# Token mean squares by a constant stationary operand: a root of 528 columns instead of a root of five and a spreading by transposition

## The chip, the cores and the metric

The kernel runs on one core of a Trainium2 chip. The metric is the device time of one execution in microseconds (us); lower is better. Times before are 818.12, 819.78 and 821.24 us, with a median of 819.78. One further execution was profiled: it took 818.42 us, and the profile's span, from its first instruction to its last, is 816.4 us.

## The reference

Two layers of an encoder with a residual stream of 528 tokens (512 of a grid, 16 meta tokens) by 1024 features. What matters here is the norm at the start of each layer, the projection behind it, and the norm of each head's queries and keys:

```
def rms_norm(x, g):
    xf = x.astype(jnp.float32)
    y = xf * lax.rsqrt(jnp.mean(xf * xf, axis=-1, keepdims=True) + EPS)
    return (y * g.astype(jnp.float32)).astype(x.dtype)

h = rms_norm(x, norm_g)
proj = jnp.einsum('bld,de->ble', h, w_in)
qa, ka, va, za, qb, kb, vb, zb, ga, gb = split_cols(proj)
qa = apply_axial_rope(rms_norm(qa.reshape(b, l, ATTN_HEADS, HEAD_DIM), q_norm_g), cos, sin)
ka = apply_axial_rope(rms_norm(ka.reshape(b, l, ATTN_KV_HEADS, HEAD_DIM), k_norm_g), cos, sin)
```

After that come grouped-query attention over all tokens (branch A), attention over windows of the grid (branch B), gates, output products and the residual sum; behind the second layer a last norm.

## The kernel before, in words

Activations lie with features on the 128 partitions and tokens along the row, 528 columns. Weights come from memory in halves of 128x512 (`weights`, L294): ScalarE rounds each to `whi` (L303), GpSimd subtracts to get the rest, `wlo` (L304). Both have five buffers, so a new half waits until TensorE has finished with the one five places earlier. A product (L379) takes two halves for each block of 128 output columns: per 128 rows of weights three matmuls, `whi` by the high part of the activations, `whi` by the low part, `wlo` by the high part (L388 to L390). In layer 0 a product runs in two spans, columns 0 to 256 and 256 to 528, each in its own bank of `pp`, of which there are two; in layer 1 most products have one span of 512 columns, but those for keys and values still have two. Layer 0's first three products are made in another way while the input arrives (L509).

The order of projections in a layer is QA to QA+3 (queries of branch A), KA (keys), VA (values), and then KB, QB, VB, ZB and ZA for each of four pairs of heads of branch B, then the gates.

The projections are made of the not yet normalized activations times the gain `norm_g`. The inverse root of the mean square of each token is multiplied in when a product leaves PSUM: `rbc`, 128x528, holds it for each token (column), the same on all partitions. Queries and keys of branch A don't use it: each head has a norm of its own, so the token's factor cancels, except that EPS must be added with the right weight, and for that the mean square itself, `mx`, is needed again.

This is how `rbc` comes about before the change:

- The squares of the features are summed over the eight tiles of features, and `norm_split` (L631) splits the sum, 128x528, into a high and a low part, `ssh` and `ssl`.
- `norm_root` calls `inverse_rms` (L433). For each of five blocks of 128 tokens, the last one overlapping the fourth, the slice of `ssh`, and then of `ssl`, is the stationary operand and the constant `mean_d` (128x2, each element 1/1024) is the moving one (L441). Tokens come out on the partitions. VectorE adds EPS (L445), which gives `mx`, 128x5; GpSimd raises it to the power -0.5 (`rsqrt`, L264 to L267), which gives `rx`, 128x5.
- `norm_spread` (L643) turns `rx` back: five transposes of one column broadcast over 128 (L646, L649), and two copies of ScalarE out of PSUM into `rbc` (L647, L650).

The head norms are near it: `sum_squares` (L537) accumulates the squares of the queries and keys into `mh` in PSUM, ten rows of 528 columns. `head_means` (L698) copies them out as `msb`, `head_roots` (L702) transposes that into `mt`, five blocks of 128 tokens by ten heads, adds `mx` times EPS (L712), and takes the roots, those of the keys by the power on GpSimd and those of the queries by Newton steps on VectorE.

What sets the order: each engine has one queue and runs it in order. `tick` (L373) is called after each span of a product, and in layer 1 also in the middle of one, and emits what is due; `NORM_AT` (L42) says after how many ticks the parts of the norm come. On top of that `BEHIND` (L66) lists pairs "this instruction behind that one" for each engine's queue, and `queue_order` (L106) puts them in as dependencies that wait for nothing and only fix the order. SP's pairs are for its DMA queue. `meta_columns` (L637), four small copies on GpSimd (`qmt`), is tied behind the root.

Of the kernel before, what the change touches and what calls it, by code (L numbers as in the profile page):

```python
# [11 lines left out]
F32 = mybir.dt.float32  # L12
# [6 lines left out]
P = 128  # L19
# [19 lines left out]
NA_AT = ({"stages": (0, 2, 4, 5, 5, 7), "values": (3, 4), "divide": (3, 4, 7)},  # L39
         {"stages": (0, 2, 4, 5, 5, 7), "values": (3, 4), "divide": (3, 4, 7)})  # L40

NORM_AT = ({"tokens": (0, 2, 4), "squares": (1, 1, 2, 3, 2), "heads": (2, 3, 5, 7, 6), "values": (1, 4)},  # L42
           {"tokens": (1, 3, 5), "squares": (2, 2, 2, 3, 2), "heads": (2, 3, 5, 7, 6), "values": (1, 4)})

PAIR_AT = (16, 32, 48)
GQA_AT_TICK, NA_AT_TICK = (0, 0), (1, 1)
# [19 lines left out]
BEHIND = {  # L66
    "Activation": (
# [5 lines left out]
    ),  # L73
    "DVE": (
# [6 lines left out]
    ),  # L81
# [11 lines left out]
    ),  # L93
    "Pool": (
        ("KB1_20", 0, "za1_0", 0), ("ga0", 7, "wlo0_24_0", 0), ("ga0", 51, "wlo1_36_1", 0), ("ga0", 52, "wlo1_36_1", 0),
        ("wl6KB", 1, "gb0", 0), ("wlo0_17_1", 0, "zb0_1", 0), ("wlo0_21_0", 0, "ga0", 10), ("wlo1_38_1", 0, "zb1_3", 0),
    ),
    "SP": (
        ("KB0_21", 0, "KB0_21", 1), ("KB0_30", 0, "QB0_3a", 1), ("P0_1_0", 1, "P0_1_0", 3), ("P1_0_0", 1, "P1_0_0", 3),
        ("Q20_1", 2, "KB0_11", 0), ("QB0_3a", 0, "QB0_3a", 1), ("raw1_46_0", 0, "bias1_7", 0), ("turn1_2_1", 0, "QB1_2a", 0),  # L100
        ("turn1_4_1", 0, "bias1_7", 0),
    ),
}
# [52 lines left out]
def trunk_kernel(ctx: ExitStack, tc: tile.TileContext, xT, w, gn, gf, bias, rope, out):  # L156
# [28 lines left out]
    def bank(pool, name, tag):  # L185
        return pool.tile([P, 512], F32, tag=tag, name=name)
# [77 lines left out]
    def rsqrt(out, x):  # L264
        with tc.high_priority():
            e = minus_half.unsqueeze(2) if len(x.shape) == 3 else minus_half
            return nc.gpsimd.tensor_tensor(out, x, e.to_broadcast(list(x.shape)), op=ALU.pow)  # L267
# [157 lines left out]
    def token_tiles(n):  # L425
        return [P * t for t in range(4)] + ([LAST] if n > NREAL else [])
# [3 lines left out]
        split(sh[:, :n], sl[:, :n], ss[:, :n])  # L430
        return sh, sl

    def inverse_rms(ss, n, name):  # L433

        tt = token_tiles(n)
        k = len(tt)
        sh, sl = ss
        ps = bank(ps_t, f"ms{name}", "tp")
        for t, a in enumerate(tt):
            for i, v in enumerate((sh, sl)):  # L440
                nc.tensor.matmul(ps[:, 2 * t:2 * t + 2], v[:, a:a + P], mean_d, start=i == 0, stop=i == 1)  # L441
        mx = tiny.tile([P, 5], F32, tag="mx", name=f"mx{name}")
        rx = tiny.tile([P, 5], F32, tag="rx", name=f"rx{name}")
        with tc.high_priority():
            nc.vector.tensor_scalar_add(mx[:, :k], ps[:, :2 * k].rearrange("p (t i) -> p t i", i=2)[:, :, 0], EPS)  # L445
        return mx, rx, rsqrt(rx[:, :k], mx[:, :k])


    pieces, xs, h, done = {}, [], [], [None, None]
# [72 lines left out]
    for l in range(DEPTH):  # L522
# [109 lines left out]
            st["ss"] = split_squares(total["ss"], NTOK, f"{l}")  # L632

        def norm_root():
            st["mx"], st["rx"], st["root"] = inverse_rms(st["ss"], NTOK, f"{l}")

        def meta_columns():  # L637

            with tc.issue_after(st["root"].ins):
                for j in range(4):  # L640
                    nc.gpsimd.tensor_copy(qmeta[:, j], qs[j][:, NREAL:])

        def norm_spread():  # L643
            ps = bank(ps_t, f"rb{l}", "tp")
            for t in range(4):
                nc.tensor.transpose(ps[:, P * t:P * (t + 1)], st["rx"][:, t:t + 1].to_broadcast([P, P]), ident)  # L646
            nc.scalar.copy(rbc[:, :NREAL], ps)  # L647
            ps = bank(ps_t, f"rbm{l}", "tp")
            nc.tensor.transpose(ps[:, :P], st["rx"][:, 4:5].to_broadcast([P, P]), ident)  # L649
            nc.scalar.copy(rbc[:, NREAL:], ps[:, P - NMETA:P])  # L650

        Q2, qmeta = [None] * 8, tiny.tile([P, 4, NMETA], F32, tag="qmt", bufs=1, name=f"qmt{l}")

# [6 lines left out]
        for j in range(4):  # L660
            q, rotate = rotated(QA + j, g_q[l], full, "q")
            qs.append(q)

            if l == 0:
                turns.append(rotate)
            else:
                with tc.issue_after(evac["low"].ins):
                    rotate()
                if j > 1:
                    stack_pair(j - 2)  # L670
            if l == 0 and j == 3:
                turns[0]()
            if l == 0 and j == 1:

                with tc.issue_after(evac["last"].ins):
                    norm_split()
                evac["last"] = split_at["hi"]
            if j == 0:
                for after, part in zip(NORM_AT[l]["tokens"], (norm_split, norm_root, norm_spread)):
                    if after:  # L680
                        side_gqa.later(after, part)
                if full:
                    side_gqa.later(4, meta_columns)
# [13 lines left out]

        def head_means():  # L698
            st["msb"] = slot("G", f"msb{l}")
            nc.scalar.copy(st["msb"][:10], joined(mps)[:10])  # L700

        def head_roots():  # L702

            ps = bank(ps_a, f"mt{l}", "avn")
            for t, a in enumerate(token_tiles(NTOK)):
                nc.tensor.transpose(ps[:, 10 * t:10 * t + 10], st["msb"][:10, a:a + P], ident[:10, :10])
            mh = tiny.tile([P, 50], F32, tag="mh", bufs=1, name=f"mh{l}")
            rh = tiny.tile([P, 50], F32, tag="rh", bufs=1, name=f"rh{l}")
            m3, st["r3"] = (t.rearrange("p (t c) -> p t c", t=5) for t in (mh, rh))
            p3 = ps[:, :50].rearrange("p (t c) -> p t c", t=5)  # L710
            e3 = st["mx"].unsqueeze(2).to_broadcast([P, 5, 10])
            nc.vector.scalar_tensor_tensor(m3, e3, EPS, p3, op0=ALU.mult, op1=ALU.add)  # L712
            rsqrt(st["r3"][:, :, 8:10], m3[:, :, 8:10])

            r, x = (t[:, :, 0:8] for t in (st["r3"], m3))
            tm = tiny.tile([P, 5, 8], F32, tag="tmh", bufs=1, name=f"tmh{l}")
            nc.vector.tensor_scalar(r.bitcast(I32), x.bitcast(I32), -0.5, float(0x5f3759df), op0=ALU.mult, op1=ALU.add)
            with tc.issue_after(newton(r, x, tm).ins):
                st["fk"] = pair_factors(slice(0, 4), slice(8, 10), 4, "k")
                st["fm"] = pair_factors(slice(4, 5), slice(8, 10), 1, "km")  # L720
            for _ in range(2):
                newton(r, x, tm)
            st["r8"] = tiny.tile([P, 4, 8], F32, tag="r8", name=f"r8_{l}")
            nc.vector.tensor_scalar_mul(st["r8"], r[:, 0:4], 0.125)
# [660 lines left out]
```

## Time and profile before

| what | value |
|---|---|
| median of three runs | 819.78 us |
| profiled execution, time | 818.42 us |
| profiled execution, span | 816.4 us |
| TensorE (PE) busy | 808.9 us |
| VectorE (DVE) busy | 505.5 us |
| ScalarE (ACT) busy | 473.6 us |
| GpSimd (POOL) busy | 418.5 us |
| mean granted clock of TensorE | 0.999 |

How to read what is quoted below. In the page, an engine's line gives its busy time, the share of the span and the number of instructions; then comes the chain of work that ended last. A list of waits has the instruction that waited, what it waited for, and us in total, times, longest us. In the answers for one line of the kernel the three numbers after the count are the shortest, median and longest duration in ns, then the first and last start. In a timeline each row has the start in us from the start of the span, the length in us, engine, line, operation, output and inputs, shapes and count, and in brackets how long the engine had been idle before it and what ended that. L304 is line 304 of the kernel before. Names such as `wlo` or `rx` are those of the program's tiles, without buffer numbers. A matmul's row lasts longer than its share of the engine, since matmuls overlap: the time that it takes is the distance to the start of the next one.

### The profile page before, as it was taken

To read this page: it belongs to the slowest core of one execution; us is meant where nothing else is said; L and a number is where in the kernel's file an instruction comes from. 1 tells how busy PE (TensorE), PEld (TensorE's weight loads), DVE (VectorE), ACT (ScalarE), POOL (GpSimd) and SP (SyncE) were. 2 spreads that over 40 slices of the span, in tenths; PEclk is the share of its full clock that TensorE was granted. 3 is DMA by queue.
4 is the path that set the end of the run, shared out by engine and by line. 5 is a ranking of instruction groups with operands and counts; after the bars stand their busy time and mean duration, and the time that the engine had idled before them with its cause. 6 is when DMAs were issued, how large, how long until landed. Compare 5 with 4: busy or idle time off the path is not lost.

```text
span 816.4 us, 16080 instructions
## 1 busy us (share of the span) xinstructions
PE 808.9 (99%) x5658; PEld 755.5 (93%) x5658; DVE 505.5 (62%) x1154; ACT 473.6 (58%) x1137; POOL 418.5 (51%) x362
## 2 busy tenths in 40 slices
PE   9999999999999999999999999999999999999997
PEld 9999999999999999999998989898988888888886
DVE  7566767796785662456447667676867655344633
ACT  7745677577865664433445557566848755544322
POOL 1654454454553544655764645454725555545750
PEclk9999999999999999999999999999999999999999
DMA  8347574667555563425555584767774555652502
GB/s 299 105 130 210 154 203 134 186 214 203 178 157 181 160 211 118 151 97 172 145 128 133 139 240 135 212 172 189 192 226 162 171 179 155 192 192 90 194 1 104
DMA packets 113248, 134.99 MB, mean 165 GB/s; under 512 B 31888, under 2 KB 66192, under 8 KB 113168
## 3 DMA queue, kind: packets, MB, share of 16 engines
q1 hardware_dynamic: 112448, 132.90, 54.7%
q8 instruction: 45, 0.74, 0.4%
q10 hardware_dynamic: 720, 1.06, 0.3%
q14 instruction: 35, 0.29, 0.1%
HBM read 98.50 MB, written 21.84 MB: 147 GB/s over the span
## 4 chain that ended last, share of the span: by engine, by line
PE 93%; DMA 3%; SPq 1%; issue 1%; DVE 1%; ACT 0%; POOLq 0%; POOL 0%; DVEq 0%
PE pp L390 20%; PE pp L389 20%; PE pp L388 20%; PE av L974 4%; PE y L388 4%; PE y L390 4%; PE y L389 4%; PE avb L1121 2%; PE S L624 2%; PE S L625 2%; PE pf L1305 2%; PE pf L1303 2%; PE pf L1304 2%; PE pp L513 1%; PE Sb L625 1%; PE Sb L624 1%
## 5 line engine op out<-in xcount | busy, mean ns | idle before, releaser
L304 POOL TENSOR_TENSOR wlo<-raw,whi 128x512 fp32r<-128x512 f32 x210 | 285.7, 1370 | 283.2 <-ACT whi L303 224.3
L388 PE MATMUL pp<-hh,whi 128*128 128x256 f32 (+2 forms) x1040 | 325.2, 313 | 0.0
L390 PE MATMUL pp<-hh,wlo 128*128 128x256 f32 (+2 forms) x1040 | 324.3, 312 | 0.0
L389 PE MATMUL pp<-hl,whi 128*128 128x256 f32 (+2 forms) x1040 | 323.4, 311 | 0.0
L390 PEld LDWEIGHTS pp<-hh,wlo 128*128 128x128 f32 x1040 | 195.7, 188 | 10.2
L389 PEld LDWEIGHTS pp<-hl,whi 128*128 128x128 f32 x1040 | 195.7, 188 | 9.4
L388 PEld LDWEIGHTS pp<-hh,whi 128*128 128x128 f32 x1040 | 195.8, 188 | 8.7
L303 ACT CAST whi<-raw 128x512 fp32r<-128x512 f32 x210 | 127.9, 618 | 104.8 <-PE pp L389 42.2
L967 POOL TENSOR_TENSOR ga<-pm,ga 32x128 fp32r<-32x128 f32 x64 | 39.1, 612 | 62.3 <-ACT ga L965 38.4
L936 DVE STREAM_TRANSPOSE P<-P 128x512 f32<-128x512 f32 x64 | 46.3, 725 | 28.5 <-ACT P L910 28.0
L1200 DVE TENSOR_TENSOR mg<-pp,rbc 128x256 f32<-128x256 f32 (+2 forms) x48 | 24.7, 515 | 48.8 <-PE pp L390 48.4
L906 DVE CUSTOM_DVE_ANT_0 P<-S,r 128x528 f32<-128x528 f32 x64 | 44.8, 700 | 14.0 <-PE S L625 13.2
L257 DVE TENSOR_TENSOR ptl<-P,pth 128x512 fp32r<-128x512 f32 x64 | 49.0, 781 | 4.8 <-ACT pth L256 4.2
L910 ACT ACTIVATE P<-P,st 128x528 f32<-128x528 f32 x64 | 47.2, 737 | 1.7
L1061 ACT ACTIVATE bias<-bias,stb 128x208 f32<-128x208 f32 (+1 forms) x64 | 31.0, 485 | 17.9 <-DVE stb L1059 17.8
L1201 ACT ACTIVATE mg<-mg 128x256 f32<-128x256 f32 (+2 forms) x48 | 23.6, 492 | 29.9 <-DVE mg L1200 29.5
L256 ACT CAST pth<-P 128x512 fp32r<-128x512 f32 x64 | 39.3, 613 | 0.9 <-DMA P<-turn 0.8
L389 PE MATMUL pp<-mx,whi 128*128 128x272 f32 (+1 forms) x128 | 36.4, 285 | 0.0
L388 PE MATMUL pp<-mx,whi 128*128 128x272 f32 (+1 forms) x128 | 36.4, 285 | 0.0
L390 PE MATMUL pp<-mx,wlo 128*128 128x272 f32 (+1 forms) x128 | 36.4, 285 | 0.0
L909 ACT ACTIVATE st<-st 128x1 f32<-128x1 f32 x64 | 12.9, 202 | 39.5 <-DVE st L906 38.9
L974 PE MATMUL av<-pth,VA 128*128 128x256 f32 x128 | 34.0, 288 | 0.0
(534 smaller groups left out, 1718.2 us busy)
## 6 DMA issues: line engine op xcount, KB each, us to landing
raw<-in_w_dram SPq DMA_DIRECT2D x210, 256.0 KB
turn<-P SPq DMA_DIRECT2D x32, 528.0 KB
P<-turn SPq DMA_DIRECT2D x128, 128.0 KB
bias<-in_bias_dram SPq DMA_DIRECT2D x16, 480.0 KB
KB<-KB SPq DMA_DIRECT2D x24, 272.0 KB
rawl<-in_w_dram SPq DMA_DIRECT2D x16, 256.0 KB
x<-in_xT_dram SPq DMA_DIRECT2D x8, 264.0 KB
xr<-in_xT_dram SPq DMA_DIRECT2D x8, 264.0 KB
```

The lines of the kernel that those rows point to most:

```text
L256: split_at["hi"] = nc.scalar.copy(hi, src)
L257: split_at["any"] = nc.vector.tensor_sub(lo, src, hi.bitcast(F32))
L303: cast = nc.scalar.copy(hi, raw)
L304: sub = nc.gpsimd.tensor_sub(lo, raw, hi.bitcast(F32))
L388: nc.tensor.matmul(ps, wh, rh[:, a:b], start=i == 0, stop=False)
L389: nc.tensor.matmul(ps, wh, rl[:, a:b], start=False, stop=False)
L390: nc.tensor.matmul(ps, wl, rh[:, a:b], start=False, stop=i == n - 1)
L906: newest["max"] = nc.vector.tensor_tensor_reduce(p[:n], joined(S)[:n], scale[:n].to_broadcast([n, NTOK]), 1.0, -3e38, ALU.mult, ALU.max, s ...
L910: nc.scalar.activation(p[:n], p[:n], AF.Exp, bias=st[:n, 1:2], scale=1.0, accum_out=st[:n, 2:3] if total is None else total)
L936: nc.vector.transpose(c["both"][:n, a:b], c["both"][:n, a:b])
L967: nc.gpsimd.tensor_sub(tm[64 + 32 * t:96 + 32 * t, n * t:n * (t + 1)], m, tm[:32, :n].bitcast(F32))
L974: nc.tensor.matmul(c["av"], rows2(c["t"][i][0]), c["t"][i][1], start=i == 0, stop=i == 8)
```

## The change

`inverse_rms` no longer brings tokens to partitions. The constant, broadcast to 128x128, is the stationary operand, and `ssh` and `ssl` are the moving ones: four matmuls, for columns 0 to 256 and 256 to 528. The mean square of a token then stands in its column on all 128 partitions. VectorE adds EPS in two instructions into `m`, 128x528, a tile of the tag "G" (eight buffers shared with other work), and GpSimd raises all 528 columns to the power -0.5 straight into `rbc`. `norm_spread` and its two ticks go. The mean squares for the heads' EPS are now added in `head_means`, on VectorE, where ScalarE made a plain copy before, and in `head_roots` a copy takes the place of that addition. The list of pairs is a new one.

```diff
-NORM_AT = ({"tokens": (0, 2, 4), "squares": (1, 1, 2, 3, 2), "heads": (2, 3, 5, 7, 6), "values": (1, 4)},
-           {"tokens": (1, 3, 5), "squares": (2, 2, 2, 3, 2), "heads": (2, 3, 5, 7, 6), "values": (1, 4)})
+NORM_AT = ({"tokens": (0, 2), "squares": (1, 1, 2, 3, 2), "heads": (2, 3, 5, 7, 6), "values": (1, 4)},
+           {"tokens": (1, 3), "squares": (2, 2, 2, 3, 2), "heads": (2, 3, 5, 7, 6), "values": (1, 4)})
...
-    def inverse_rms(ss, n, name):
-
-        tt = token_tiles(n)
-        k = len(tt)
-        sh, sl = ss
-        ps = bank(ps_t, f"ms{name}", "tp")
-        for t, a in enumerate(tt):
-            for i, v in enumerate((sh, sl)):
-                nc.tensor.matmul(ps[:, 2 * t:2 * t + 2], v[:, a:a + P], mean_d, start=i == 0, stop=i == 1)
-        mx = tiny.tile([P, 5], F32, tag="mx", name=f"mx{name}")
-        rx = tiny.tile([P, 5], F32, tag="rx", name=f"rx{name}")
-        with tc.high_priority():
-            nc.vector.tensor_scalar_add(mx[:, :k], ps[:, :2 * k].rearrange("p (t i) -> p t i", i=2)[:, :, 0], EPS)
-        return mx, rx, rsqrt(rx[:, :k], mx[:, :k])
+    def inverse_rms(ss, r, name):
+
+        m = slot("G", f"mx{name}")
+        for a, b in ((0, CUT), (CUT, NTOK)):
+            ps = bank(ps_t, f"ms{name}_{a}", "tp")[:, :b - a]
+            for i, v in enumerate(ss):
+                nc.tensor.matmul(ps, mean_d[:, :1].to_broadcast([P, P]), v[:, a:b], start=i == 0, stop=i == 1)
+            with tc.high_priority():
+                nc.vector.tensor_scalar_add(m[:, a:b], ps, EPS)
+        return m, rsqrt(r[:, :NTOK], m)
...
-            st["mx"], st["rx"], st["root"] = inverse_rms(st["ss"], NTOK, f"{l}")
+            st["mx"], st["root"] = inverse_rms(st["ss"], rbc, f"{l}")
...
-        def norm_spread():
-            ps = bank(ps_t, f"rb{l}", "tp")
-            for t in range(4):
-                nc.tensor.transpose(ps[:, P * t:P * (t + 1)], st["rx"][:, t:t + 1].to_broadcast([P, P]), ident)
-            nc.scalar.copy(rbc[:, :NREAL], ps)
-            ps = bank(ps_t, f"rbm{l}", "tp")
-            nc.tensor.transpose(ps[:, :P], st["rx"][:, 4:5].to_broadcast([P, P]), ident)
-            nc.scalar.copy(rbc[:, NREAL:], ps[:, P - NMETA:P])
...
-            nc.scalar.copy(st["msb"][:10], joined(mps)[:10])
+            nc.vector.scalar_tensor_tensor(st["msb"][:10], st["mx"][:10], EPS, joined(mps)[:10], op0=ALU.mult, op1=ALU.add)
...
-            p3 = ps[:, :50].rearrange("p (t c) -> p t c", t=5)
-            e3 = st["mx"].unsqueeze(2).to_broadcast([P, 5, 10])
-            nc.vector.scalar_tensor_tensor(m3, e3, EPS, p3, op0=ALU.mult, op1=ALU.add)
+            nc.vector.tensor_copy(mh, ps[:, :50])
```

Of the pairs, those that bear on the instructions spoken of below (the rest of the list is of the same kind: some pairs gone, some new, one name of a `cmb` tile counted anew):

```diff
     "DVE": (
+        ("k0_4", 1, "va0", 1), ("k0_4", 1, "va0", 2), ("va0", 1, "msb0", 0), ("za1_3", 0, "ptl1_3_1_0", 0),
...
     "Pool": (
+        ("qmt0", 0, "wlo0_14_1", 0),
-        ("wlo1_38_1", 0, "zb1_3", 0),
...
     "SP": (
-        ("KB0_21", 0, "KB0_21", 1),
+        ("KB0_10", 0, "QB0_1a", 0), ("KB0_10", 0, "QB0_1a", 1), ("P0_5_0", 2, "P0_5_0", 3),
+        ("sumsb1_1", 1, "bias1_4", 0), ("sumsb1_3", 0, "sumsb1_3", 1), ("thereb1_1", 1, "KB1_20", 0), ("thereb1_1", 3, "KB1_20", 0),
```

More of the change, by code (lines that the diff above doesn't have):

```diff
@@ L95 @@
         ("KB1_20", 0, "za1_0", 0), ("ga0", 7, "wlo0_24_0", 0), ("ga0", 51, "wlo1_36_1", 0), ("ga0", 52, "wlo1_36_1", 0),
-        ("wl6KB", 1, "gb0", 0), ("wlo0_17_1", 0, "zb0_1", 0), ("wlo0_21_0", 0, "ga0", 10), ("wlo1_38_1", 0, "zb1_3", 0),
+        ("qmt0", 0, "wlo0_14_1", 0), ("wl6KB", 1, "gb0", 0), ("wlo0_17_1", 0, "zb0_1", 0), ("wlo0_21_0", 0, "ga0", 10),
     ),
     "SP": (
-        ("KB0_21", 0, "KB0_21", 1), ("KB0_30", 0, "QB0_3a", 1), ("P0_1_0", 1, "P0_1_0", 3), ("P1_0_0", 1, "P1_0_0", 3),
-        ("Q20_1", 2, "KB0_11", 0), ("QB0_3a", 0, "QB0_3a", 1), ("raw1_46_0", 0, "bias1_7", 0), ("turn1_2_1", 0, "QB1_2a", 0),
[4 rows of a table added]
         ("turn1_4_1", 0, "bias1_7", 0),
@@ L678, in trunk_kernel @@
             if j == 0:
-                for after, part in zip(NORM_AT[l]["tokens"], (norm_split, norm_root, norm_spread)):
+                for after, part in zip(NORM_AT[l]["tokens"], (norm_split, norm_root)):
                     if after:
```

36 rows, old and new, of the table BEHIND are left out of this document.

## The prediction

> **What bounds the kernel now.** I read the profile's page first, then the list of what TensorE (PE) waited for.
>
> ```profile
> span 816.4 us, 16080 instructions
> PE 808.9 (99%) x5658; PEld 755.5 (93%) x5658; DVE 505.5 (62%) x1154; ACT 473.6 (58%) x1137; POOL 418.5 (51%) x362
> ...
> PE 93%; DMA 3%; SPq 1%; issue 1%; DVE 1%; ACT 0%; POOLq 0%; POOL 0%; DVEq 0%
> ```
>
> ```profile
> PE warm L200 <- PEq L1373: 0.8, 1, 0.8
> PE pp L513 <- DVE hh L405: 0.2, 1, 0.2
> PE pp L513 <- ACT hh L407: 0.2, 1, 0.2
> PE avb L1121 <- DVE na L867: 0.2, 1, 0.2
> ```
>
> PE is busy for 808.9 of 816.4 us, the chain that ended last is 93% PE, and all its waits together are 1.4 us. So PE sets the end. Work taken from PE is time won, one for one; work on the other engines costs nothing until PE has to wait for it. GpSimd (POOL) is only half busy, but it makes `wlo`, the low half of every weight, and so PE can be made to wait for it. This change puts one large instruction there, so I looked up next what the root costs on POOL: the instructions of line 267, and as a comparison POOL's add of squares.
>
> ```profile
> L267 POOL TENSOR_TENSOR sums<-sums,minus_half x4: 552/569/664, 795.6 to 811.6; 128x1 f32<-128x1 f32 x4
> L267 POOL TENSOR_TENSOR rx<-mx,minus_half x2: 1187/1374/1562, 32.0 to 435.0; 128x5 f32<-128x5 f32 x2
> L267 POOL TENSOR_TENSOR rh<-mh,minus_half x2: 1954/1962/1970, 48.9 to 459.6; 128x10 f32<-128x10 f32 x2
> ```
>
> ```profile
> L422 POOL TENSOR_TENSOR sq<-sq,sq x6: 1767/1771/1787, 384.9 to 414.2; 128x528 f32<-128x528 f32 x6
> ```
>
> The power is not priced like the add. One column takes 569 ns, five take 1187 (the faster of the two), ten take 1962: (1187 - 569)/4 = 154.5 ns a column, and (1962 - 1187)/5 = 155. It is a straight line of 414 ns + 155 ns a column, with no sign of columns being worked on side by side. The add handles 528 columns in 1771 ns.
>
> **The change part by part.** Everything around the root, layer 0 first, then layer 1, in the timeline of PE:
>
> ```profile
> 30.50 0.16 PE L441 MATMUL ms<-means_r,ssh 128*128 128x2 f32 x1
> ...
> 31.53 0.28 PE L540 MATMUL mh<-qh,means_r 128*10 128x256 f32 x1
> ...
> 32.02 0.28 PE L388 MATMUL pp<-hh,whi 128*128 128x256 f32 x1
> ...
> 37.84 0.60 PE L646 MATMUL rb<-ident,rx 128*128 128x128 f32 x4
> ...
> 38.30 0.36 PE L388 MATMUL pp<-hh,whi 128*128 128x256 f32 x1
> 38.50 0.29 PE L389 MATMUL pp<-hl,whi 128*128 128x256 f32 x1
> ...
> 41.24 0.28 PE L540 MATMUL mh<-qh,means_r 128*10 128x256 f32 x1
> ...
> 45.45 0.28 PE L390 MATMUL pp<-hh,wlo 128*128 128x256 f32 x1
> ```
>
> ```profile
> 432.26 0.16 PE L441 MATMUL ms<-means_r,ssh 128*128 128x2 f32 x1
> ...
> 433.29 0.48 PE L388 MATMUL pp<-hh,whi 128*128 128x512 f32 x1
> ...
> 439.40 0.60 PE L646 MATMUL rb<-ident,rx 128*128 128x128 f32 x4
> ...
> 439.87 0.48 PE L388 MATMUL pp<-hh,whi 128*128 128x512 f32 x1
> ...
> 442.73 0.28 PE L540 MATMUL mh<-qh,means_r 128*10 128x256 f32 x1
> ...
> 449.30 0.28 PE L390 MATMUL pp<-hh,wlo 128*128 128x256 f32 x1
> ```
>
> *PE.* Removed: the ten matmuls of two columns, 30.50 to 31.53, 1.03 us; the five spreading transposes, 37.84 to 38.30, 0.46 us, and 0.08 us by which the matmul behind them starts its successor late (0.20 us instead of about 0.12). Added: four matmuls of 256, 256, 272 and 272 moving columns; the four `mh` matmuls from 31.53 to 32.02 have these shapes and take 0.49 us. Net -1.08 us a layer (layer 1 has the same rows: 1.03 and 0.47), -2.2 us in all.
>
> *VectorE and ScalarE.* Both are idle 38% of the span or more, so their changed work costs nothing by itself: two additions out of PSUM for one (about 0.42 us each, by the `va` row below), two copies of `rbc` less, one copy of 10x528 moved from ScalarE to VectorE. Without that cover they would be about 1 us a layer. *The pairs* reorder instructions inside engines and on the DMA queues (on SP they move pair transfers and the reads of sums behind others, all prefetched while PE waits for none). PE waits 1.4 us in all, so they can win at most that; they lose nothing while no wait reaches PE. I take zero, +-1.4 us.
>
> *The root.* Its stage, in the timelines of POOL, VectorE and ScalarE:
>
> ```profile
> 19.64 3.04 POOL L304 TENSOR_TENSOR wlo<-raw,whi 128x512 fp32r<-128x512 f32 x2 [17.04 <-ACT whi L303]
> 24.58 1.31 POOL L304 TENSOR_TENSOR wlo<-raw,whi 128x512 fp32r<-128x512 f32 x1 [1.90 <-ACT whi L303]
> 27.87 3.78 POOL L304 TENSOR_TENSOR wlo<-raw,whi 128x512 fp32r<-128x512 f32 x3 [1.98 <-ACT whi L303]
> 31.95 1.19 POOL L267 TENSOR_TENSOR rx<-mx,minus_half 128x5 f32<-128x5 f32 x1 [0.30 <-PE mh L540]
> 33.09 0.33 POOL L641 COPY qmt<-q 128x16 f32<-128x16 f32 x2
> 33.37 1.30 POOL L304 TENSOR_TENSOR wlo<-raw,whi 128x512 fp32r<-128x512 f32 x1
> ```
>
> ```profile
> 434.96 1.56 POOL L267 TENSOR_TENSOR rx<-mx,minus_half 128x5 f32<-128x5 f32 x1 [0.70 <-DVE mx L445]
> 436.86 1.30 POOL L304 TENSOR_TENSOR wlo<-raw,whi 128x512 fp32r<-128x512 f32 x1 [0.34 <-DMA x1d<-xt]
> ```
>
> ```profile
> 32.23 0.71 DVE L562 TENSOR_TENSOR ql<-qs,qh 128x528 fp32r<-128x528 f32 x1 [0.36 <-ACT qs L560]
> ...
> 33.66 1.57 DVE L568 TENSOR_TENSOR qr<-qr,sin 128x528 f32<-128x528 f32 x1
> ...
> 42.30 0.41 DVE L770 TENSOR_TENSOR va<-pp,rbc 128x256 f32<-128x256 f32 x1
> ```
>
> ```profile
> 434.73 0.15 DVE L445 TENSOR_SCALAR mx<-ms 128x5 f32<-128x5 f32 x1
> ```
>
> ```profile
> 436.17 0.62 ACT L303 CAST whi<-raw 128x512 fp32r<-128x512 f32 x1 [3.28 <-PE pp L389]
> ```
>
> No row of before shows a root of 528 columns. Its floor is the add of that shape, 1.8 us; the line gives 1.962 + 518 x 0.155 = 82.1 us. In between lies the lowest slope that any two rows allow, (1954 - 1562)/5 = 78 ns, which gives 1.954 + 518 x 0.078 = 42.6 us. I take 82.1: all three sizes are rows of this very instruction, and lie on one line, while the add is another operation. The extrapolation, from 10 columns to 528, is the weak point.
>
> Two things stand behind the root. POOL works in order, so the next `wlo` waits, and the `qmt` copies with it. VectorE works in order too, and its first product with `rbc` (42.30) waits, with everything behind it; PE then finds no free bank of `pp`, which has two.
>
> Layer 0: the second addition ends at about 31.8, POOL is free at 31.65, so the root runs from 31.9 to 114.0, and the next `wlo` is done at 115.3. The weights of KA and VA are split by then (six `wlo` stand ahead of the root: two at 19.64, one at 24.58, three here). PE runs on through them to the first matmul of KB that reads `wlo`, 45.45, now 1.08 earlier: 44.4. It stalls for 115.3 - 44.4 = 70.9 us. (Were that one `wlo` ahead of the root, PE would wait for the bank instead, to the same microsecond.)
>
> Layer 1: VectorE is free at 434.73, two additions bring it to 435.6, the root ends at 517.7, the `wlo` behind it at 519.0. That one (436.86 now) is the eleventh of the layer, for VA's first half: there are five buffers, each `wlo` waits for PE to free one, and its cast comes at 436.17, when the second half of QA+2 is done. PE gets as far as VA's third matmul, 449.30 - 1.08 = 448.2, and stalls for 70.8 us. All times of layer 1 shift alike with what layer 0 costs.
>
> Afterwards POOL owes no more than it did before at the same place of PE, since PE stood still as long, and at 51% busy it has room; I add nothing for the restart.
>
> The profiled execution took 818.4 us, 2.0 over its span and 1.4 below the median, 819.8. Sum: 818.4 - 2.2 + 70.9 + 70.8 = 957.9; in terms of the median, 959.
>
> The Trainium skill, TensorE: Matmul & The Clock Gate, Part 1, says that PE's clock falls to half after some 3.4 us without work and needs as long to return; by it each stall costs an estimated 1.7 us more, and the sum would be 962. No row quoted here has PE pausing that long.
>
> **Rivals.**
>
> *The root is hidden (not slower).* It runs at the pace of POOL's other two-input work, 528 columns in 1.8 us (the row of `sq`), is done by 33.7, long before 42.30, and only PE's -2.2 is left: 816.2, or 818 as a median, no change that can be measured (0.5%, about 4 us, is what a measurement of this kernel can tell). It decides at (44.4 - 31.9 - 1.3)/528 = 21 ns a column: below it nothing stalls. Against it stand three sizes at 155 ns. The Trainium skill, GPSIMD Engine Reference, section 3.1, prices GpSimd's elementwise work at about 2.6 cycles of its 1.2 GHz clock per element, an estimated 1.1 us for 528, which is this rival; the rows of the power disagree, 155 ns against its 2.2.
>
> *The line flattens.* A long contiguous row could be handled better than five or ten columns. At 78 ns a column the root ends 39.5 us sooner in each layer: 959 - 79 = 880. Nothing in the rows shows it.
>
> *VectorE is shut out as well.* At 33.66 a product of two SBUF tiles took 1.57 us, where one of that shape took 0.71 at 32.23: POOL's `wlo` ran from 33.37 to 34.67. If the root does the same for all of its time, VectorE stops at the `ql` of 32.23, and PE at the `mh` that needs it: at 41.24 instead of 45.45, and in layer 1 at 442.73 instead of 449.30. That is 10.8 us more: 970. Against it: that 0.71 us lay wholly inside the five-column root of 31.95 to 33.14. But five columns may be read at once, and 528 not. The Trainium skill, SBUF — State Buffer, section Who interferes with whom, has the rule: a VectorE instruction with two SBUF inputs and a GpSimd instruction that reads SBUF shut each other out for a whole instruction. The row at 33.66 agrees, the one at 32.23 does not.
>
> *The change does nothing that counts*, because the root is not on the path for a reason I don't see: 819.
>
> **How the numbers follow.** Forecast, root near 82 us and two stalls near 71: 0.55, 959. VectorE shut out: 0.20, 970. Flatter line: 0.10, spread from 820 to 940, with about half of it above 878. Hidden: 0.13, 818. Nothing: 0.02. The low end is the flat line at its measured lowest slope, 880 less 1.4 for the pairs: 878. The high end is 970, plus about 0.75 us for each of some ten products of VectorE in a layer that hold POOL up (the root of 435.0 took 1562 against 1187): 985. That holds 0.55 + 0.20 + 0.05 = 0.80. Slower by over 0.5%: 0.86 (the first three, and a little). Within 0.5%: 0.11. Faster: 0.03, hidden with pairs that win their all.
>
> **What would show it.** Right: line 267 has two rows of 128x528 on POOL at about 82 us; POOL's busy time rises by some 160 us; PE's busy digits drop to nothing in two stretches of some 71 us, one after each mean; PE's list of waits names `wlo` on POOL, or VectorE's `va`, for about 70 us twice. The shut-out shows as VectorE products of 80 us beside the root. Wrong: rows of a few us at line 267, with PE as busy as before. If the root is long and PE still runs, then I have misread what stands behind it.

## The result, and the profile after

The changed kernel takes 968.4 us (median of six runs, 967.4 to 969.7) against 820.5 us (818.1 to 822.7): a ratio of 1.180, 95% interval 1.178 to 1.183. Executions of the kernel before spread over some 6 us (818.8 to 824.6 in 23 of them), the longest at a mean granted clock of 0.995, the shortest at 1.000, so a difference of 2 us between medians is soft. The profiled execution took 968.46 us, its span is 966.4. The page of the changed kernel, beside that of before:

```profile
span 966.4 us, 16028 instructions
## 1 busy us (share of the span) xinstructions
PE 810.6 (84%) x5636; PEld 757.0 (78%) x5636; DVE 510.2 (53%) x1158; ACT 471.6 (49%) x1131; POOL 582.5 (60%) x362
## 2 busy tenths in 40 slices
PE   9700199999999999999997002999999999999997
...
POOL 2999965444535444554768999645545555555660
PEclk9955599999999999999999555999999999999999
...
PE 78%; POOL 9%; issue 9%; DVE 1%; ACT 1%; DMA 1%; SPq 0%; POOLq 0%; DVEq 0%
```

TensorE's busy time is nearly what it was, 810.6 us for 808.9. The span has grown around it: PE's row has two holes, one early in each layer, and in both POOL's row shows a 9. POOL stands in the chain that ended last, where it had 0%. What PE waited for most, in the changed kernel (us in total, times, longest):

```profile
PE pp L394 <- DVE va L761: 74.2, 1, 74.2
PE pp L396 <- POOL wlo L310: 73.6, 1, 73.6
```

Two waits hold 147.8 us. The first is a matmul that needs the bank of `va`, the second one that needs a `wlo`. POOL's timeline shows what stood ahead of both, here in layer 0 and, in the second fence, in layer 1:

```profile
26.95 5.04 POOL L310 TENSOR_TENSOR wlo<-raw,whi 128x512 fp32r<-128x512 f32 x4 [1.96 <-ACT whi L309]
31.95 85.12 POOL L273 TENSOR_TENSOR rbc<-mx,minus_half 128x528 f32<-128x528 f32 x1
117.04 0.46 POOL L643 COPY qmt<-q 128x16 f32<-128x16 f32 x3
117.46 1.82 POOL L310 TENSOR_TENSOR wlo<-raw,whi 128x512 fp32r<-128x512 f32 x1
```

```profile
511.91 85.01 POOL L273 TENSOR_TENSOR rbc<-mx,minus_half 128x528 f32<-128x528 f32 x1 [1.31 <-DVE mx L447]
596.89 6.21 POOL L310 TENSOR_TENSOR wlo<-raw,whi 128x512 fp32r<-128x512 f32 x5
```

In layer 0 four `wlo` stand in the group ahead of the root, where before had three: the one for KB's first half was already split, and so the product with `rbc` is what PE waited for. In layer 1 it is the `wlo`. VectorE beside the root, in layer 0:

```profile
33.98 0.70 DVE L571 TENSOR_TENSOR q<-q,cos 128x528 f32<-128x528 f32 x1
34.71 0.71 DVE L572 TENSOR_TENSOR q<-q,qr 128x528 f32<-128x528 f32 x1
38.12 0.71 DVE L564 TENSOR_TENSOR kl<-ks,kh 128x528 fp32r<-128x528 f32 x1 [2.70 <-ACT ks L562]
...
117.11 0.42 DVE L761 TENSOR_TENSOR va<-pp,rbc 128x256 f32<-128x256 f32 x1 [77.03 <-POOL rbc L273]
```

Products of two SBUF tiles run at about their usual 0.70 us while the root is under way (0.67 to 0.78 for the five that start beside it in layer 0); then VectorE idles 77 us for `rbc`.

The last few microseconds are in PE's rows after each hole. Layer 0:

```profile
117.59 0.58 PE L394 MATMUL pp<-hh,whi 128*128 128x256 f32 x1 [74.24 <-DVE va L761]
...
118.40 0.41 PE L394 MATMUL pp<-hh,whi 128*128 128x256 f32 x1
118.61 0.41 PE L395 MATMUL pp<-hl,whi 128*128 128x256 f32 x1
```

A matmul of 256 columns now starts every 0.21 us. In before it was 0.12, and it is again in the second span of this product. In the table of stretches of the changed kernel (length, busy time of PE, its weight loads, DVE, ACT and POOL, then the granted clock, of which 1.00 is full speed, the DMA share and GB/s) the clock falls some five microseconds into the hole, and is low when PE starts again:

```profile
47.00:48.00 1.00, 0.00 (x0) 0.00 (x0) 0.00 (x0) 0.00 (x0) 1.00 (x1) 1.00 0.00 0
48.00:49.00 1.00, 0.00 (x0) 0.00 (x0) 0.00 (x0) 0.00 (x0) 1.00 (x1) 0.77 0.00 0
49.00:50.00 1.00, 0.00 (x0) 0.00 (x0) 0.00 (x0) 0.00 (x0) 1.00 (x1) 0.50 0.00 0
...
122.50:123.50 1.00, 1.00 (x8) 0.78 (x7) 0.39 (x2) 0.00 (x0) 1.00 (x2) 0.50 0.91 324
123.50:124.50 1.00, 1.00 (x9) 0.97 (x10) 0.70 (x4) 0.16 (x1) 1.00 (x2) 0.93 0.49 156
```

### The profile page after: what moved, and what is told of

It reads as the page before. It is cut to its first block, busy times and chain, and to the rows that moved or that the text cites. A ratio compares the mean times of both kernels' runs of the same rounds, so it can differ in the third digit from the quotient of the medians.

```text
span 966.4 us, 16028 instructions
## 1 busy us (share of the span) xinstructions
PE 810.6 (84%) x5636; PEld 757.0 (78%) x5636; DVE 510.2 (53%) x1158; ACT 471.6 (49%) x1131; POOL 582.5 (60%) x362
## 4 chain that ended last, share of the span: by engine, by line
PE 78%; POOL 9%; issue 9%; DVE 1%; ACT 1%; DMA 1%; SPq 0%; POOLq 0%; DVEq 0%
PE pp L396 17%; PE pp L394 17%; PE pp L395 16%; POOL rbc L273 8%; PE av L965 3%; PE y L394 3%; PE y L396 3%; PE y L395 3%; PE avb L1112 2%; PE S L626 2%; PE S L627 2%; PE pf L1296 1%; PE pf L1294 1%; PE pf L1295 1%; PE pp L515 1%
## 5 line engine op out<-in xcount | busy, mean ns | idle before, releaser
L394 PE MATMUL pp<-hh,whi 128*128 128x256 f32 (+2 forms) x1040 | 326.9, 314 | 74.2 <-DVE va L761 74.2
L396 PE MATMUL pp<-hh,wlo 128*128 128x256 f32 (+2 forms) x1040 | 326.1, 314 | 73.6 <-POOL wlo L310 73.6
L273 POOL TENSOR_TENSOR rbc<-mx,minus_half 128x528 f32<-128x528 f32 x2 | 170.1, 85067 | 1.3 <-DVE mx L447 1.3
```

What stands on the lines that cost most here:

```text
L394: nc.tensor.matmul(ps, wh, rh[:, a:b], start=i == 0, stop=False)
L396: nc.tensor.matmul(ps, wl, rh[:, a:b], start=False, stop=i == n - 1)
```

## The experiments

Nine kernels. Eight are compared by their times with the kernel before, run on the same chip in the same rounds; the first was executed once, and only its rows are used. The theory is that of the prediction: GpSimd pays for the power by the column, and TensorE stands still for all of it beyond a cover of some 11 us, the part of the root during which TensorE still has work that lies ready. Against it stood a flatter price for long rows, VectorE being shut out, and costs in the rest of the change. In all of them the `cmb` tiles are numbered by a counter of their own, so that the pairs keep meeting the same tiles.

**The price by itself.** Behind the last root of the kernel before:

```diff
+    behind = split_at["end"].ins
+    for n in (1, 2, 5, 10, 20, 40, 80, 160, 264):
+        with tc.issue_after(behind):
+            behind = rsqrt(idle[:, :n], eighth.to_broadcast([P, n])).ins
...
```

> The kernel before, with powers on GpSimd behind its last root, unread, of 1, 2, 5, 10, 20, 40, 80, 160 and 264 columns, then a product of 264 columns, then a power of 264 columns on 32 partitions only. Prices of the disputed operation by itself, at a time when VectorE has ended. Theory (a straight line in the columns): 0.41 us + 0.155 to 0.160 a column, so 0.57, 3.6, 6.7, 12.9 to 13.2, 25.2 to 26 and 41.3 to 42.7 us for 1, 20, 40, 80, 160 and 264; the product about 0.9 us; 32 partitions as long as 128. Rival (VectorE's traffic stretched the root in the changed kernel, and the price alone is the 155 of the small sizes): 41.3 for 264, where the theory's upper end has 42.7. Rival (the line flattens for long rows): under 35 for 264.

The groups of POOL in this run, by shape (busy us, mean ns):

```profile
L274 POOL TENSOR_TENSOR idle<-eighth,minus_half 128x264 f32<-128x264 f32 x1 | 42.4, 42435 | 0.1
L1351 POOL TENSOR_TENSOR idle<-eighth,minus_half 32x264 f32<-32x264 f32 x1 | 42.4, 42425 | 0.1
...
L274 POOL TENSOR_TENSOR idle<-eighth,minus_half 128x160 f32<-128x160 f32 x1 | 25.8, 25815 | 0.1
L274 POOL TENSOR_TENSOR idle<-eighth,minus_half 128x80 f32<-128x80 f32 x1 | 13.1, 13106 | 0.1
...
L274 POOL TENSOR_TENSOR idle<-eighth,minus_half 128x10 f32<-128x10 f32 x1 | 1.9, 1950 | 0.1
...
L1349 POOL TENSOR_TENSOR idle<-idle,eighth 128x264 f32<-128x264 f32 x1 | 0.6, 626 | 0.1
```

It is a straight line to the end, but for a slope that grows from 155 to 160 ns: (42435 - 25815)/104 = 159.8 ns a column, (25815 - 13106)/80 = 158.9. Nothing flattens, and a quarter of the partitions costs the same, so the price is of columns and not of elements. A product of the same 264 columns takes 0.63 us, a 68th. VectorE is at rest here (its last row ends before 815 us, the powers run from 814 to 954), and the row is 42.4 us for 264 columns, not the rival's 41.3: the step from 155 to 160 ns belongs to the longer row, and VectorE's traffic did not make it. Twice this row, less one start-up, is 84.5 us for 528 columns; the 85.1 of the changed kernel leaves 0.6 for anything else.

**Half the columns, and a fifth.** 264, then 112 columns by the power, the others on VectorE. With 264 VectorE makes three Newton steps; with 112 it makes the first guess alone and leaves the steps out. The edit for 264:

```diff
-        return m, rsqrt(r[:, :NTOK], m)
+        root = rsqrt(r[:, :264], m[:, :264])
...
+        return m, root
```

> The changed kernel with 264 of the 528 columns left to GpSimd's power, and the other 264 made on VectorE by Newton steps. Theory (a price per column, to be paid in full as soon as it is longer than the cover): the root takes 0.41 + 264 x 0.160 = 42.7 us instead of 85.1, each stall shrinks by 42.4 us to about 32, and the time is 968.4 - 84.8 = 884 us. Rival (a long row costs something of its own, such as a start-up that is paid once): root well over 43 us, time over 900. Rival (price as in the add): root of 1 us, no stall, 818.

Measured: 884.6 us (ratio 1.078, 1.076 to 1.080). The waits of PE and the root's rows in this run:

```profile
PE pp L400 <- DVE va L774: 31.7, 1, 31.7
PE pp L402 <- POOL wlo L316: 31.5, 1, 31.5
```

```profile
L279 POOL TENSOR_TENSOR rbc<-mx,minus_half x2: 42517/42680/42843, 32.9 to 470.3; 128x264 f32<-128x264 f32 x2
```

> The changed kernel with 112 columns left to GpSimd's power, and the first guess alone on VectorE for the other 416, Newton steps left out. Theory (price 0.41 + 0.1595 a column, cover about 11 us, as the run with 264 columns had stalls of 31.6 under a root of 42.6): root 18.3 us, two stalls of about 7.3 us, and up to 2 us for each restart, so 14.6 to 19 us over the run with the first guess only, 833 to 838. Rival (below some length other work of TensorE fills the gap): within 3 us of the run with the first guess only.

Measured: 834.1 us (1.017, 1.014 to 1.019), 18.1 over the run with the first guess only (816.0, below):

```profile
PE pp L400 <- DVE va L770: 7.5, 1, 7.5
PE pp L402 <- POOL wlo L316: 6.5, 1, 6.5
```

```profile
L279 POOL TENSOR_TENSOR rbc<-mx,minus_half x2: 18225/18294/18364, 32.0 to 444.1; 128x112 f32<-128x112 f32 x2
```

Roots of 85.1, 42.7 and 18.3 us have stalls of 73.9, 31.6 and 7.0 us: the difference is 11.2, 11.1 and 11.3 us. That is the cover, and beyond it every microsecond of the root is one of the kernel's. The stalls are not all: of the 17.7 us between the spans of the run with 112 columns and the run with the first guess only, 14.0 are the two stalls and 3.4 are PE's busy time (809.8 for 806.4), at a clock of 0.50 after each.

**Only the queue, with `rbc` on time.** The kernel before, with two unread roots behind its own:

```diff
+        root = rsqrt(rx[:, :k], mx[:, :k])
+        for _ in range(2):
+            with tc.issue_after(root.ins):
+                root = rsqrt(idle, eighth.to_broadcast([P, 264]))
```

> The kernel before, with its own root of five columns and its spreading, and two roots of 264 columns put behind that root on GpSimd in each layer, whose result nobody reads (about 85 us a layer). rbc is on time here, and only GpSimd's queue is held up. Theory (either of the two things behind the root would hold TensorE by itself): TensorE waits for wlo in both layers, in two parts with one wlo between the unread roots, altogether about 75 and 74 us, and the time is 819 + 149 + about 4 for restarts = 971. Rival (only the product with rbc holds TensorE, and the weights' lead covers GpSimd's absence): 818 to 825.

Measured: 973.6 us (1.187, 1.185 to 1.189).

```profile
PE pp L397 <- POOL wlo L311: 145.7, 3, 73.3
```

Nobody reads these roots, and PE stands still as long: the weights behind them are enough. That the product with `rbc` can hold PE by itself is seen in layer 0 of the changed kernel, where the `wlo` that PE needed was ready, and, with GpSimd's queue free, in the next run, where PE waits 4.8 us for the bank of a late `va`. The expected 971 was missed by 3 us: PE was busy for 816.8 us, 7.9 more than before, where about 4 were expected for restarts. The clock was at 0.50 after each of the three holes, and once more after a pause of only 2 us:

```profile
722.46 0.38 PE L635 MATMUL S<-KA1h,Q 128*128 128x256 f32 x1 [1.96 <-DVE stb L1070]
```

```profile
722.50:723.00 0.50, 0.50 (x4) 0.50 (x5) 0.50 (x1) 0.50 (x3) 0.00 (x0) 1.00 0.23 78
...
723.50:724.00 0.50, 0.50 (x5) 0.50 (x4) 0.47 (x2) 0.47 (x1) 0.00 (x0) 0.50 0.02 8
```

**The root on VectorE.** All 528 columns by the integer guess and three Newton steps:

```diff
-        return m, rsqrt(r[:, :NTOK], m)
+        root = None
+        tmp = slot("G", f"nt{name}")
+        y, x, t = (v[:, 0:NTOK] for v in (r, m, tmp))
+        with tc.high_priority():
+            nc.vector.tensor_scalar(y.bitcast(I32), x.bitcast(I32), -0.5, float(0x5f3759df), op0=ALU.mult, op1=ALU.add)
+            for _ in range(3):
+                last = newton(y, x, t)
+        return m, root or last
```

> The changed kernel with the root of 528 columns taken from GpSimd and made on VectorE: an integer first guess and three Newton steps, ten instructions of 128x528, as the kernel does already for the query heads. Everything else of the change stays: the four matmuls, no spreading, the additions out of PSUM, the new pairs. Theory (the length of GpSimd's root is the whole loss): TensorE no longer stands still; what is left is the 1.08 us a layer that the matmuls win, so 818 us against 820.5, between 816 and 820. Rival (something else of the change costs as well: the constant as stationary operand, the tile held in G, the additions on VectorE, the new pairs): over 823 us.

Measured: 828.9 us (1.011, 1.009 to 1.012). The holes are gone, but the expected 816 to 820 was missed. Its waits:

```profile
PE pp L400 <- DVE va L774: 5.8, 2, 4.8
PE mt L712 <- DVE msb L706: 1.7, 1, 1.7
PE mh L555 <- DVE ql L577: 0.9, 1, 0.9
```

The scheduler interleaved the ten instructions with the rotations of the queries and keys, and `va` came at 47.73 us instead of 42.30. PE's waits are not the whole miss: beside the run with the first guess only, below, they are 8.4 us longer, and PE's busy time is 4.4 us longer (810.8 for 806.4), since the clock fell to 0.50 after the wait of 4.8 us and again after the one of 1.7. So the number did not tell whether the rest of the change costs something. To tell, I took the Newton steps out:

> The changed kernel with only the integer first guess of the root, one instruction of VectorE over 528 columns; the Newton steps are left out, so rbc is a few per cent off. Nothing is long here and nothing is late: it shows what the rest of the change is worth. In the run with all Newton steps TensorE waited 8.4 us more than before, on VectorE, whose ten instructions were interleaved with the rotations and ended late. Theory (the rest of the change is the 2.2 us that the matmuls win): 818.5 us against 820.8, ratio 0.997, TensorE's waits below 2 us. Rival (the rest costs something): 821 or more.

Measured: 816.0 us (0.994, 0.992 to 0.996), with these waits, and PE busy for 806.4 us:

```profile
PE warm L212 <- PEq L1373: 0.8, 1, 0.8
PE av L974 <- DVE ptl L269: 0.7, 1, 0.7
PE pp L524 <- DVE hh L417: 0.3, 1, 0.3
PE avb L1121 <- ACT P L910: 0.2, 1, 0.2
```

The rest of the change costs nothing; it wins 5.1 us by the medians (821.1 before), more than the 2.2 us of the matmuls. The next run says where the remainder is from.

> As the run with the first guess only, but with the list of pairs of the kernel before. Theory (the pairs hide nothing here): within 1.4 us of the run with the new list. Rival (the new list is needed for the new places of the norm's parts): 822 or more.

Measured with the list of pairs of before: 818.8 us (0.998, 0.996 to 0.999), 817.6 to 820.8, while the new list gave 815.7 to 816.3. So the new pairs are worth about 2.8 us here, twice the 1.4 that I had expected at most, and the matmuls about 2 (2.3 by the medians, 1.8 by PE's busy time in the profiles, 807.1 for 808.9). Where those 2.8 us sit is only in part settled: between the two profiles PE's waits differ by 1.1 us (one wait of 1.0 of a score's product for VectorE is gone), its busy time by 0.7, the spans by 1.9. PE's waits were 1.4 us in the kernel before, are 3.1 here with the old list and 2.0 with the new one, so the old list suits the changed order less well than it suited its own.

**Versions to use.** Two Newton steps, and the rotations of the keys, in layer 0 also those of the first queries, behind the root:

> A version meant to be used: the change with the root on VectorE, two Newton steps after the first guess (an error of about 5 in a million is left in rbc), and in layer 0 the rotations of the first queries and the keys ordered behind the root. Theory (VectorE's lateness was all that the run with three interleaved steps lost): va's product comes at about 42 us, TensorE's waits below 3 us, 818 to 820 us against 820.8, at best a gain that a measurement barely tells. Rival (seven instructions of 0.7 us are still too late somewhere in layer 0 or 1): 822 to 826.

Measured: 823.1 us (1.002, 1.001 to 1.004): the rival's number. PE waited 3.1 us for `msb`, 0.9 for a `ql`. In the second version ScalarE makes the squares, `msb` has priority, and the rotations stay where the change has them:

```diff
...
+            for _ in range(2):
+                nc.scalar.activation(t, y, AF.Square)
+                nc.vector.scalar_tensor_tensor(t, t, -0.5, x, op0=ALU.mult, op1=ALU.mult)
+                last = nc.vector.scalar_tensor_tensor(y, t, 1.5, y, op0=ALU.add, op1=ALU.mult)
...
```

> A second version meant to be used: two Newton steps of which ScalarE makes the square, so that VectorE has five instructions of 128x528 for the root instead of seven, and msb of the head means gets priority on VectorE, since TensorE waited for it in the version with seven. Theory (VectorE's lateness in the two stages is what these versions lose against the run with the first guess only): waits on VectorE of about 2 us more than with the first guess only, 817 to 820 us against 821, ratio 0.995 to 0.999. Rival (the two crossings between the engines in each layer make rbc later than seven instructions in a row): 822 or more.

Measured: 818.1 us against 819.8 (0.998, interval 0.997 to 0.999). It beats both kernels, the one before by a hair; of the 5 us that the first guess alone shows to be there, the steps give most back. Beside the priority of `msb` it differs from the changed kernel in the two Newton steps that replace the power; the error of a few in a million that they leave in `rbc` is estimated and was not measured.

## Why the prediction was right, step by step

- *PE sets the end, and nothing hides a wait of PE.* Right: of 150.0 us between the two profiled executions (968.46 - 818.42) PE's two waits are 147.8.
- *PE's own work, -2.2 us.* Right: 806.4 us busy with the first guess only, against 808.9, is -2.5; the four matmuls take 0.49 us from 29.60 to 30.09 us, as the `mh` rows said.
- *The root, 82.1 us by a line through one, five and ten columns.* The mechanism was right over fifty times the range; the slope was a little low, 155 ns for 160, and the root took 85.1. This is the mis-sized term: 3.0 us a layer. (By the slope as it is written there, 0.155, the sum is 82.3; the 82.1 goes with 154.8, and the difference counts for nothing.) The rivals that it be hidden, or flatter, fall with the row of 264 columns. The rule of the Trainium skill, GPSIMD Engine Reference, section 3.1, of about 2.6 cycles per element, fits the product (626 ns for 264 columns, an estimated 572 by the rule) and not the power (42435).
- *What stands behind the root.* Right in both halves: GpSimd's queue held PE by itself with the unread roots, and a late product with `rbc` held it by itself, for 4.8 us, with the root on VectorE. In layer 0 it was the bank and not the `wlo`, which the prediction had named as equal. PE stopped at 43.35, one microsecond before the expected 44.4, and went on at 117.6 for 115.3.
- *Two stalls of 70.9 and 70.8.* 74.2 and 73.6: 6.1 us more, of which the root's length makes 5.9. In layer 0 two further errors nearly cancel: PE stopped 1 us sooner, and what stands between the root and PE, a product of 0.42 us, is shorter than the `wlo` of 1.3.
- *Nothing added for the restart.* Wrong by 4.2 us: PE busy was 810.6 with the holes and 806.4 without. The clock of 0.50 after each hole, up to 123.5 us in layer 0 and 601.4 in layer 1, is the cause that the traces show. The Trainium skill, TensorE: Matmul & The Clock Gate, Part 1, said so, and the estimate from it was 1.7 us a stall; the trace agrees in kind, with 2.1 on average. The sum by that rule, 962, was nearer than the forecast's 959.
- *VectorE shut out, 970.* The time came within 2 us of this rival and yet it was not the mechanism: products of about 0.70 us ran beside the root, and PE was not held at the `mh` matmuls. 6 us of longer root and 4 us of low clock made the same sum. The rule of the Trainium skill, SBUF — State Buffer, section Who interferes with whom, shows beside this power in one product only, of 1.44 us right after the start of layer 1's root; all others that started beside the two roots took 0.67 to 0.78. Why that one was longer is open. Beside a `wlo` the rule agrees, as the first of these rows of layer 1 shows, under the `wlo` of 509.31 to 510.60; the other two are under the root of 511.91:

```profile
509.39 1.76 DVE L570 TENSOR_TENSOR qr<-qr,sin 128x512 f32<-128x512 f32 x1
...
512.46 1.44 DVE L572 TENSOR_TENSOR q<-q,qr 128x512 f32<-128x512 f32 x1
...
515.91 0.69 DVE L570 TENSOR_TENSOR qr<-qr,sin 128x512 f32<-128x512 f32 x1
```

- *The pairs, +-1.4 us.* Mis-sized: about 2.8 us in their favour, by the two runs with the first guess only. The bound was PE's waits in the old order, and the new order has others with the old list (3.1 us). That is shown without the power alone; under the two stalls the pairs' part was not measured.
- *The range.* The measured time lies well inside. The high end's 0.75 us for each product that holds GpSimd up is twice what the quoted rows show (1562 - 1187 is 375 ns), and nothing of that kind was seen beyond the 0.6 us that the price leaves.

Together: -2.5 + 147.8 + 4.2 + 0.5 for other idle time of PE gives the 150.0; forecast were 139.5.

## What to carry to other kernels

Price an operation by rows of the same operation at two or three sizes, and look for what it scales with: a form that spares work on the bound engine can turn five columns into 528, and where the price is per column and blind to partitions, bringing the tokens to the partitions is what the transposes were paying for. Before putting a long instruction on an idle engine, count what is queued behind it: half-idle POOL had only 11 us of cover here. When a substitute is tested, test it once with the disputed part left out, or its own lateness is taken for a cost of the rest. Add a term for the clock behind each pause of the bound engine: it was 4 us for the two holes here, and elsewhere a pause of 2 us was followed by a low clock too.

## What the runs showed of the hardware

The power on GpSimd costs 0.41 us plus 0.155 to 0.160 us per column, on 32 partitions as on 128 (42.43 and 42.44 us for 264 columns). In both holes of the changed kernel TensorE's granted clock stayed at 1.00 for some five microseconds after its last matmul and then fell to 0.50. That is no fixed time: it was 2.1 and 2.9 us in the run with the unread roots (from 45.4 to 47.5 and from 525.8 to 528.75) and 3.4 in the run with three Newton steps. In these two runs it also fell within 1.5 us of the end of a pause of 1.96 and of 1.75 us, when TensorE was at work again; in the run with two Newton steps it did not fall after a pause of 1.8. After the holes of the changed kernel it came back after about 6 us of matmuls in layer 0, and 3.2 us in layer 1, where the spacing returns from 0.21 to 0.12 us at 601.5.
